# Feed-forward outputs: the last six chunks as plain products, block by block, and slots at multiples of 128 bytes

## The chip, the cores and the metric

The kernel runs on one core of a Trainium2 chip. The metric is device time in microseconds (us) of one execution. Three runs of the kernel before took 1276.67, 1276.96 and 1278.26 us; the median is 1276.96 us. One more execution was profiled, and all rows below come from it.

## The reference, cut to what matters

Two decoder layers work on 512 positions of width 1024. Layer 0 mixes with gated linear attention (GLA), layer 1 with a gated DeltaNet (GDN). Each layer ends with a gated feed-forward network (FFN) with a short causal convolution, and each sublayer closes with a scaled residual and a LayerNorm:

```python
def conv_ffn(x, w_in, conv_w, w_out):
    h = causal_dwconv(x @ w_in, conv_w)
    gate, up = jnp.split(h, 2, axis=-1)
    return (jax.nn.gelu(gate, approximate=False) * up) @ w_out

h = layer_norm(ALPHA * h + conv_ffn(h, ffn_w_in[i], ffn_conv_w[i], ffn_w_out[i]),
               ln_g[i, 1], ln_b[i, 1])
```

`w_in` is 1024 x 5632 and `w_out` 2816 x 1024, so the hidden width has 22 chunks of 128. Everything is float32.

## The kernel before, in words

Each float32 operand of a large product is split into a high part (rounded to the matmul format fp32r) and a low remainder. A product is then three matmuls: high by high, high by low, low by high. ScalarE writes the high part and VectorE the low part (`split_out`, L533). A 128x512 matmul of this kind is the unit of nearly all TensorE work here.

The 512 positions are four blocks of 128 (`tb` 0 to 3), and the width 1024 is two halves of 512 (`hf` 0 and 1), so the residual is eight tiles `h[tb][hf]`. The normed input stands transposed in `xh` and `xl`.

The FFN (`ffn`, L802) goes through the 22 hidden chunks in groups of 8, 8 and 6. Within a group, `fm_items` (L422) computes per chunk a gate and an up product, 24 matmuls each ("fm" in the trace). ScalarE and VectorE apply the convolution (`ffn_conv`, L794), the Gelu and the product with the gate. Then the group's part of the output product follows in `folded` (L850, "fold" in the trace): chunks are taken in pairs and the positions and the output width in halves, which makes each pair a 2x2 block product, and this is done with seven half-size products rather than eight. So a pair costs 7 forms x 2 row blocks x 3 terms = 42 matmuls. VectorE builds the four sums of activations (L831 to L834) and the sums of weights (L347), and seven updates (L877) add the products to the residual. The stationary operands are slices of tiles `fh` and `fl`, the moving ones the weight tiles `wh` and `wl`.

After the last group each residual block is normed as soon as both its halves are complete. In layer 0 that is `ln` (L689): statistics, two halves normed in place, eight transposes on TensorE ("xT"), then the new `xh` and `xl`. In layer 1 it is `ln_out` (L736), which scales and writes the output. The order of the seven products makes blocks 2 and 3 complete before 0 and 1. The next mixer therefore begins with the positions of blocks 2 and 3 (`self.halves = (1, 0)`, L908): its first four products (`HEADSTART`) are done for 256 positions at a time.

The instruction order on TensorE is written by a planner in the kernel: a model clock (`self.clk`) and background tasks that `pump` inserts when their time comes. Weights are taken from a plan list by `weight`, which prefetches as many items ahead as `self.look` says. Weights come through three buffers `raw` and are split into four pairs `wh`, `wl`, or, where the plan says so (`in_slots`), into free slots of the stage's own pool ("wsh", "wsl"). The mixers' output products (`out_proj`, L486) use that last way in their second half.

In SBUF the tiles `xh`, `xl`, `h`, `raw`, `wh` and `wl` begin at multiples of 128 bytes in each partition. The stage pools lie behind the constants, and their slots and the tiles `form`, `fh`, `fl` and `folded` begin 32 bytes past such a multiple.

Of the kernel before, what the change touches and what calls it, by code (L numbers as in the profile page):

```python
# [8 lines left out]
F32 = mybir.dt.float32  # L9
# [6 lines left out]
P = 128  # L16
# [44 lines left out]
class Trunk:  # L61
# [3 lines left out]
    def __init__(self, ctx, tc):  # L65
        self.tc = tc
        self.nc = nc = tc.nc
        self.n = 0
        ec = ctx.enter_context
        ap = ec(tc.tile_pool(name="acts", bufs=1))  # L70
        self.xh = ap.tile([P, NC, S], F32R, name="xh", tag="xh")
        self.xl = ap.tile([P, NC, S], F32R, name="xl", tag="xl")
        self.wp = ec(tc.tile_pool(name="wts", bufs=WB))
        self.hp = ec(tc.tile_pool(name="resid", bufs=2 * NTB))
        self.rp = ec(tc.tile_pool(name="raws", bufs=RAWB))
        self.cp = ec(tc.tile_pool(name="const", bufs=1))
        self.sp = ec(tc.tile_pool(name="small", bufs=4))
        self.pp = ec(tc.tile_pool(name="ps", bufs=8, space=bass.MemoryType.PSUM))
        self.dp = ec(tc.tile_pool(name="scratch", bufs=1, space=bass.MemoryType.DRAM))
        self.mp = None  # L80
        self.stage("gla", SLOTS)
        self.resets()
        self.halves = (0, 1)
        self.ident = self.keep([P, P], "ident")
        make_identity(nc, self.ident)
        ones = self.keep([P, 32], "one")
        self.one, self.warm, self.eps = (ones[:, i:i + 1] for i in range(3))
        nc.gpsimd.memset(ones, 1.0)
        nc.gpsimd.memset(self.eps, LN_EPS)
        self.h = None  # L90
        self.plan = []
        self.issued = 0
        self.loaded = 0
        self.taken = 0
        self.held = 0
        self.look = 1
        self.pin = True
        self.ready = []
        self.dve = 0.0
        self.clk = 0.0  # L100
        self.tasks = []
        self.flags = {}
        self.tabled = None
        self.wide = None
        self.block = None
        self.next_block = 0.0
        self.late = []
        self.first = None
        self.between = None

# [17 lines left out]

    def slot(self, s, dt=F32):
        return self.mp.tile([P, S], dt, name=self.uid(s), tag="slot")  # L130

    def psum(self, s):
        return self.pp.tile([P, S], F32, name=self.uid(s), tag="bank")
# [123 lines left out]
    def issue(self, item):  # L257
# [28 lines left out]
        if self.in_slots(item):  # L286
            w = []
            for j in range(used // S):
                wh, wl = self.slot("wsh", F32R), self.slot("wsl", F32R)
                nc.scalar.copy(wh, raw[:, blk(j, S)])  # L290
                nc.vector.tensor_sub(wl, raw[:, blk(j, S)], wh)
                self.vec(0.7)
                w.append((wh, wl))
            return w
# [127 lines left out]
    def fm_items(self, items):  # L422

        start = 0 if all(self.is_set(("x", tb)) for tb in range(NTB)) else HEADSTART
        first = items[:start]
        ws, banks = [], []
        for turn, half in enumerate(self.halves if first else ()):
            self.wait(("x", 2 * half), ("x", 2 * half + 1))
            for i, f in enumerate(first):
                if not turn:  # L430
                    ws.append(self.weight())
                    banks.append(self.psum("fm"))
                self.fm_mms(banks[i], ws[i], half * 256, half * 256 + 256, self.pin and not turn and i < 2)
                if turn:
                    self.spend()
                    f(banks[i])
        for f in items[start:]:
            w = self.weight()
            ps = self.psum("fm")
            self.fm_mms(ps, w, 0, S)  # L440
            self.spend()
            f(ps)
# [43 lines left out]
    def out_proj(self, a, n, first, final, pieces=1):  # L486
# [25 lines left out]
            self.tm_half(a, n, TAIL if last else 1, done, last, pieces if last else 1)  # L512
        self.look = LOOKAHEAD


    def exp_ln_table(self):
        load = self.nc.scalar.preload_act_table_set("natural_log_exp_and_others")
# [124 lines left out]

    def ln_consts(self, g, b):
        self.lg, self.lb = self.keep([P, 4 * NC], "lg"), self.keep([P, 4 * NC], "lb")
        self.specs = [(w.rearrange("i j (c p) -> (i j c) p", p=P), 4 * NC, t)
                      for w, t in ((g, self.lg), (b, self.lb))]

# [4 lines left out]
        for tb in range(NTB):  # L652
            self.flags.pop(("x", tb), None)

    def ln_gb(self):

        if self.gb is None:
            self.gb = []
            for src in self.gb_rows:
                for hf in range(2):  # L660
                    t = self.slot("gb")
                    self.nc.sync.dma_start(t, src[blk(hf, S)].partition_broadcast(P))
                    self.gb.append(t)
        return self.gb
# [115 lines left out]
    def ffn_plan(self, w_in, w_out):  # L780
        for f0, f1 in GROUPS:
            for f in range(f0, f1):
                self.plan_fm(w_in, f * P)
                self.plan_fm(w_in, DFF + f * P)
            self.plan_fold(w_out, f0, f1)

    def ffn_consts(self, conv_w):
        cw = self.keep([P, 6 * NF], "ffn_cw" + str(len(self.specs)))
# [13 lines left out]
    def ffn(self, cw, li, g, b, final, out=False):  # L802
        nc = self.nc
        self.stage(f"ffn{li}", FFN_SLOTS)
        for gi, (f0, f1) in enumerate(GROUPS):
            act, items, forms = {}, [], []
            for f in range(f0, f1):
                def gate(ps, f=f):
                    a = self.ffn_conv(ps, cw, f, self.slot("conv"))
                    nc.scalar.activation(a, a, AF.Gelu)  # L810
                    act[f] = a

                def up(ps, f=f, f1=f1):
                    odd = (f - f0) % 2
                    if not odd:
                        t = self.mp.tile([P, 2048], F32, name=self.uid("form"), tag="form", bufs=2)
                        forms.append((t, *(self.mp.tile([P, 1792], F32R, name=self.uid(n), tag=n, bufs=4)
                                           for n in ("fh", "fl"))))
                    t, fh, fl = forms[-1]
                    u = t[:, blk(odd, S)]  # L820
                    self.ffn_conv(ps, cw, NF + f, u)
                    nc.vector.tensor_mul(u, u, act.pop(f))
                    split = lambda lo, hi: self.split_out(fh[:, lo:hi], fl[:, lo:hi], t[:, 256 + lo:256 + hi])
                    if not odd:
                        if f + 2 == f1:
                            split(0, 256)
                        return
                    if f + 1 == f1:
                        split(256, 768)
                    part = lambda i: t[:, blk(i, 256)]  # L830
                    nc.vector.tensor_sub(part(4), part(0), part(2))  # L831
                    nc.vector.tensor_sub(part(5), part(4), part(1))
                    nc.vector.tensor_sub(part(6), part(1), part(0))
                    nc.vector.tensor_add(part(7), part(5), part(3))  # L834
                    if f + 1 == f1:
                        split(768, 1792)
                    else:
                        split(0, 1792)

                items += [gate, up]  # L840
            self.fm_items(items)
            last = gi == len(GROUPS) - 1
            if last:
                self.drain()
                self.ln_begin(li, g, b)
                if out:
                    self.ln_gb()
            self.folded(forms, gi == 0, final if last else None)

    def folded(self, forms, first, final):  # L850

        nc = self.nc
        m = len(forms)
        last = final is not None
        if last:
            self.sqrt_table()
        banks = [[self.psum("fold") for _ in range(2)] for _ in range(3)]
        uses = [[n for n, _, _, at in FOLD if at == i] for i in range(3)]  # L860
        fresh = {(tb, hf) for tb in range(NTB) for hf in range(2)} if first else set()
        st = {tb: self.small([P, 2, 6], "ln_st") for tb in range(NTB)} if last else None
        done = {}

        def update(name, r, ps):
            low, high = (r, 0), (r, 1)
# [9 lines left out]
            else:  # L876
                nc.vector.tensor_tensor(h, h, ps, op)  # L877
            self.vec(0.7, self.clk + 0.4)
            done[at] = done.get(at, 0) + 1
            if last and done[at] == (1 if at == low else 2):  # L880
                nc.vector.bn_stats(st[tb][:, hf, :], h)  # L881
                self.vec(0.7)
                if all(done.get((tb, i), 0) == (1 if (tb, i) == low else 2) for i in range(2)):
                    self.st = st
                    self.spawn(final(tb))
                    self.pump()

        self.look = 3
        for name, _, form, at in FOLD:
# [14 lines left out]
                    self.pump()  # L904
                self.spend()
        self.look = LOOKAHEAD
        if last:
            self.halves = (1, 0)  # L908


    def split_y(self, y, hf, sg):
# [241 lines left out]
    def mixer_out(self, y, li, g, b, final=None):  # L1153
# [5 lines left out]
            return tuple(t[:, blk(c % 4)] for t in y[tb][hf])  # L1159

        self.out_proj(a, NC, True, self.ln)
        self.halves = (0, 1)


    def gdn_plan(self, w_in, w_out):
# [475 lines left out]
```

## Time and profile before

| | |
|---|---|
| median of three runs | 1276.96 us |
| the profiled execution, its own time | 1277.17 us |
| its span, first to last instruction | 1275.5 us |
| TensorE busy | 1244.2 us, 98% |
| VectorE busy | 951.9 us, 75% |
| ScalarE busy | 594.7 us, 47% |
| granted TensorE clock, mean | 0.992 |

A matmul's row shows a duration that overlaps with the next one, so the rate of TensorE is read from the distance between starts, not from the durations. Times in the timeline and in the chain are counted from the span's start. "PEld" is the load of a stationary operand.

### The profile page before, as it was taken

Reading aid. Unit: us, or ns where it says so; the run is one execution under the profiler, and the core shown is the slowest. Engines: PE = TensorE matmul, PEld = TensorE weight load, DVE = VectorE, ACT = ScalarE, POOL = GpSimd, SP = SyncE. Lnnn points to the kernel's source line nnn. Section 1 sums busy time; section 2 is a strip of 40 time slices with the busy share of each in tenths; the row PEclk is TensorE's granted clock in tenths of the full one; section 3 lists DMA queues with packets and bytes.
Section 4 is the critical chain, followed back from the end, with each engine's and each line's share of the span. In section 5 each row is a group of like instructions: output and inputs, shape, how many; then the busy total and the mean of one; then the engine's idle time right before and its main releaser. Section 6 shows DMA issues by size and latency. Waiting matters only on the chain.

```text
span 1275.5 us, 17191 instructions
## 1 busy us (share of the span) xinstructions
PE 1244.2 (98%) x6520; PEld 1044.7 (82%) x6520; DVE 951.9 (75%) x1593; ACT 594.7 (47%) x1064; POOL 117.2 (9%) x152
## 2 busy tenths in 40 slices
PE   8999999999999999997999999999999999999994
PEld 8878888988888888877888888988988888888873
DVE  4953556689957895896789955679589966895798
ACT  4644444544434443446765544544644434443440
POOL 4000000080000000002013120010053000000000
PEclk9999999999999999998999999999999999999997
DMA  8321224442443144114354431145352253234301
GB/s 208 111 73 60 67 94 122 143 126 79 148 133 93 60 130 123 58 42 135 103 150 113 121 75 51 50 133 149 109 156 67 87 178 99 67 101 142 119 12 66
DMA packets 170307, 132.30 MB, mean 104 GB/s; under 512 B 16360, under 2 KB 140074, under 8 KB 170224
## 3 DMA queue, kind: packets, MB, share of 16 engines
q1 hardware_dynamic: 165136, 122.05, 32.5%
q0 software_dynamic: 3888, 8.50, 2.4%
q8 instruction: 51, 0.84, 0.3%
q10 hardware_dynamic: 1200, 0.66, 0.2%
q14 instruction: 32, 0.26, 0.1%
HBM read 125.39 MB, written 5.78 MB: 103 GB/s over the span
## 4 chain that ended last, share of the span: by engine, by line
PE 90%; DVE 7%; ACT 2%; issue 1%; DMA 0%; SPq 0%; DVEq 0%; ACTq 0%
PE fm L188 50%; PE tm L188 17%; PE fold L188 13%; DVE wl L534 2%; PE o L188 2%; PE xT L205 1%; DVE h L877 1%; PE R L188 1%; PE V L188 1%; PE qkT L205 1%; PE vn L188 1%; PE pq L188 1%; PE pg L188 1%; PE yT L205 1%; DVE ln_st L881 0%
## 5 line engine op out<-in xcount | busy, mean ns | idle before, releaser
L188 PE MATMUL fm<-xh,wh 128*128 128x512 f32 (+2 forms) x1104 | 403.1, 367 | 0.7 <-ACT xh L534 0.7
L188 PE MATMUL fm<-xl,wh 128*128 128x512 f32 (+2 forms) x1104 | 400.1, 365 | 0.0
L188 PE MATMUL fm<-xh,wl 128*128 128x512 f32 (+1 forms) x1088 | 396.3, 366 | 0.0
L534 DVE TENSOR_TENSOR wl<-raw,wh 128x1024 fp32r<-128x1024 f32 (+1 forms) x166 | 206.0, 1243 | 201.5 <-ACT wh L534 201.3
L534 ACT CAST wh<-raw 128x1024 fp32r<-128x1024 f32 (+1 forms) x166 | 172.8, 1042 | 291.1 <-PE fm L188 181.1
L188 PEld LDWEIGHTS fm<-xh,wh 128*128 128x128 f32 (+1 forms) x1104 | 207.3, 189 | 33.6 <-ACT xh L534 0.9
L188 PEld LDWEIGHTS fm<-xl,wh 128*128 128x128 f32 (+1 forms) x1104 | 207.4, 189 | 32.6
L188 PEld LDWEIGHTS fm<-xh,wl 128*128 128x128 f32 x1088 | 204.5, 189 | 33.4
L188 PE MATMUL fold<-wh,fh 128*128 128x512 f32 x308 | 122.5, 401 | 8.3 <-DVE ln_t L684 6.4
L188 PE MATMUL fold<-wl,fh 128*128 128x512 f32 x308 | 122.6, 398 | 0.0
L188 PE MATMUL fold<-wh,fl 128*128 128x512 f32 x308 | 122.5, 398 | 0.0
L534 ACT CAST wh<-b 128x1024 fp32r<-128x1024 f32 x72 | 69.2, 980 | 96.4 <-PE fold L188 40.0
L534 DVE TENSOR_TENSOR wl<-b,wh 128x1024 fp32r<-128x1024 f32 x72 | 80.2, 1129 | 4.6 <-ACT wh L534 4.4
L188 PE MATMUL tm<-wh,xh 128*128 128x512 f32 x192 | 78.5, 409 | 0.8 <-ACT qk L999 0.8
L188 PEld LDWEIGHTS fold<-wh,fh 128*128 128x128 f32 x308 | 58.1, 190 | 24.9 <-issue 6.8
L188 PE MATMUL tm<-wh,xl 128*128 128x512 f32 x192 | 75.3, 392 | 0.0
L188 PE MATMUL tm<-wl,xh 128*128 128x512 f32 x192 | 75.0, 391 | 0.0
L188 PEld LDWEIGHTS fold<-wl,fh 128*128 128x128 f32 x308 | 58.4, 189 | 14.2 <-DVE wl L534 0.5
L188 PEld LDWEIGHTS fold<-wh,fl 128*128 128x128 f32 x308 | 58.3, 189 | 14.1
L799 DVE SCALAR_TENSOR_TENSOR form<-fm,ffn_cw,form 128x511 f32<-128x511 f32 x88 | 65.6, 745 | 1.8 <-ACT form L797 0.4
L799 DVE SCALAR_TENSOR_TENSOR conv<-fm,ffn_cw,conv 128x511 f32<-128x511 f32 x88 | 65.5, 744 | 1.1
L810 ACT ACTIVATE conv<-conv 128x512 f32<-128x512 f32 x44 | 27.8, 631 | 78.6 <-DVE conv L799 78.5
(286 smaller groups left out, 1700.4 us busy)
## 6 DMA issues: line engine op xcount, KB each, us to landing
raw<-in_ffn_w_in_dram SPq DMA_DIRECT2D x88, 512.0 KB, 3.9
raw<-in_gdn_w_in_dram SPq DMA_DIRECT2D x32, 512.0 KB, 4.1
b<-in_ffn_w_out_dram SPq DMA_DIRECT2D x30, 512.0 KB, 5.0
raw<-in_gla_w_in_dram SPq DMA_DIRECT2D x23, 512.0 KB, 3.7
raw<-in_ffn_w_out_dram SPq DMA_DIRECT2D x20, 512.0 KB, 3.6
raw<-in_gla_w_out_dram SPq DMA_DIRECT2D x8, 512.0 KB, 3.6
raw<-in_gdn_w_out_dram SPq DMA_DIRECT2D x8, 512.0 KB, 3.9
h<-in_x_dram SPq DMA_DIRECT2D x8, 256.0 KB, 6.2
```

The lines of the kernel that those rows point to most:

```text
L188: t = self.nc.tensor.matmul(out, a, b, start=start, stop=stop, skip_group_check=joined)
L205: t = self.nc.tensor.transpose(out, a, self.ident[:n, :n])
L534: return self.nc.scalar.copy(dst_h, src), self.nc.vector.tensor_sub(dst_l, src, dst_h)
L799: nc.vector.scalar_tensor_tensor(a[:, d:], ps[:, :S - d], tap(2 - d), a[:, d:], ALU.mult, ALU.add)
L810: nc.scalar.activation(a, a, AF.Gelu)
L877: nc.vector.tensor_tensor(h, h, ps, op)
```

## The change

The seven-product form stays for the first two groups of eight chunks. The last six chunks are computed plainly: a new function `out_rows` goes block by block, and for each block over both output halves, with 6 chunks x 3 terms = 18 matmuls each, adds the result to the residual, takes the statistics and starts the block's LayerNorm. In layer 1 the very last half is done in two pieces of 256 columns. The twelve activations' parts and the 24 weight parts of this stage stand in slices ("rooms") of the tiles `fh`, `fl` and `folded` that the second group has left. The next mixer starts with blocks 0 and 1 again, as the blocks finish in order. In layer 1 the LayerNorm's scale and bias rows stand in a `form` tile. A constant of 24 floats is added ("pad"); with it and the changed small tiles, all stage pools begin at a multiple of 128 bytes.

```diff
+    def room(self, s):
+        return self.parts.pop(0) if self.parts else self.slot(s, F32R)
...
-                wh, wl = self.slot("wsh", F32R), self.slot("wsl", F32R)
+                wh, wl = self.room("wsh"), self.room("wsl")
...
+    def out_rows(self, a, n, final, pieces):
+        nc = self.nc
+        self.sqrt_table()
+        npair = (n + 1) // 2
+        self.look = 2 * npair + WB
+        ws = []
+        self.st = [None] * NTB
+        for tb in range(NTB):
+            for hf in range(2):
+                m = pieces if tb == NTB - 1 and hf else 1
+                ps = [self.psum("tm") for _ in range(m)]
+                while len(ws) < npair * (hf + 1):
+                    ws.append(self.weight())
+                w = [t for item in ws[npair * hf:npair * (hf + 1)] for t in item]
+                if hf == 0:
+                    self.st[tb] = self.small([P, 1 + (pieces if tb == NTB - 1 else 1), 6], f"ln_st{pieces}")
+                for i in range(m):
+                    cols = blk(i, S // m)
+                    for c in range(n):
+                        self.tm_terms(ps[i][:, cols], *a(c, tb), *(t[:, cols] for t in w[c]), c == 0, c == n - 1)
+                        if c % 2:
+                            self.pump()
+                    h = self.h[tb][hf][:, cols]
+                    nc.vector.tensor_add(h, h, ps[i][:, cols])
+                    nc.vector.bn_stats(self.st[tb][:, hf + i, :], h)
+                    self.vec(1.4, self.clk + 0.4)
+            self.spawn(final(tb))
+            self.pump()
+        self.look = LOOKAHEAD
...
         self.lg, self.lb = self.keep([P, 4 * NC], "lg"), self.keep([P, 4 * NC], "lb")
+        self.keep([P, 24], "pad")
...
-            self.plan_fold(w_out, f0, f1)
+            if f1 < NF:
+                self.plan_fold(w_out, f0, f1)
+            else:
+                for hf in range(2):
+                    for f in range(f0, f1, 2):
+                        self.plan_tm(w_out, f * P, min(2, f1 - f), hf * S, True)
...
+            if last:
+                self.parts = [t[:, blk(i, S)] for _ in range(4) for t in fine() for i in range(3)]
+                for _ in range(FOLDED):
+                    t = self.mp.tile([P, 1024], F32, name=self.uid("b"), tag="folded", bufs=FOLDED)
+                    self.parts += [t[:, blk(i, S)].bitcast(F32R) for i in range(2)]
...
+                def plain(ps, f=f, f1=f1):
+                    u = self.ffn_conv(ps, cw, NF + f, self.slot("conv"))
+                    nc.vector.tensor_mul(u, u, act.pop(f))
+                    t = self.room("gh"), self.room("gl")
+                    self.split_out(*t, u)
+                    forms.append(t)
+                    if f == f1 - 3:
+                        self.look = 5
+
+                items += [gate, plain if last else up]
...
+                a = lambda c, tb: tuple(t[:, blk(tb)] for t in forms[c])
+                self.out_rows(a, f1 - f0, final, 2 if out else 1)
+            else:
+                self.folded(forms, gi == 0)
...
-        if last:
-            self.halves = (1, 0)
```

More of the change, by code (lines that the diff above doesn't have):

```diff
@@ L82, in __init__ @@
         self.resets()
-        self.halves = (0, 1)
         self.ident = self.keep([P, P], "ident")
@@ L107, in __init__ @@
         self.late = []
+        self.parts = []
         self.first = None
@@ L426, in fm_items @@
         ws, banks = [], []
-        for turn, half in enumerate(self.halves if first else ()):
+        for turn, half in enumerate((0, 1) if first else ()):
             self.wait(("x", 2 * half), ("x", 2 * half + 1))
@@ L653, in ln_begin, with ln_gb @@
             self.flags.pop(("x", tb), None)
-    def ln_gb(self):
+    def ln_gb(self, room=None):
         if self.gb is None:
@@ L660, in ln_gb @@
                 for hf in range(2):
-                    t = self.slot("gb")
+                    t = room.pop(0) if room else self.slot("gb")
                     self.nc.sync.dma_start(t, src[blk(hf, S)].partition_broadcast(P))
@@ L804, in ffn @@
         self.stage(f"ffn{li}", FFN_SLOTS)
+        fine = lambda: tuple(self.mp.tile([P, 1792], F32R, name=self.uid(n), tag=n, bufs=4) for n in ("fh", "fl"))
         for gi, (f0, f1) in enumerate(GROUPS):
             act, items, forms = {}, [], []
+            last = gi == len(GROUPS) - 1
+            if last:
[3 more added lines that the diff above has]
+                    self.parts += [t[:, blk(i, S)].bitcast(F32R) for i in range(2)]
             for f in range(f0, f1):
@@ L816, in up @@
                         t = self.mp.tile([P, 2048], F32, name=self.uid("form"), tag="form", bufs=2)
-                        forms.append((t, *(self.mp.tile([P, 1792], F32R, name=self.uid(n), tag=n, bufs=4)
-                                           for n in ("fh", "fl"))))
+                        forms.append((t, *fine()))
                     t, fh, fl = forms[-1]
@@ L826, in up @@
                             split(0, 256)
[L827 to L836, printed above, removed]
-                    else:
-                        split(0, 1792)
-                items += [gate, up]
+                    else:
+                        if f + 1 == f1:
+                            split(256, 768)
+                        part = lambda i: t[:, blk(i, 256)]
+                        nc.vector.tensor_sub(part(4), part(0), part(2))
+                        nc.vector.tensor_sub(part(5), part(4), part(1))
+                        nc.vector.tensor_sub(part(6), part(1), part(0))
+                        nc.vector.tensor_add(part(7), part(5), part(3))
+                        split(768 if f + 1 == f1 else 0, 1792)
+                def plain(ps, f=f, f1=f1):
[7 more added lines that the diff above has]
+                items += [gate, plain if last else up]
             self.fm_items(items)
-            last = gi == len(GROUPS) - 1
             if last:
@@ L846, in ffn, with folded @@
                 if out:
-                    self.ln_gb()
-            self.folded(forms, gi == 0, final if last else None)
-    def folded(self, forms, first, final):
+                    t = self.mp.tile([P, 2048], F32, name=self.uid("form"), tag="form", bufs=2)
+                    self.ln_gb([t[:, blk(i, S)] for i in range(4)])
+                a = lambda c, tb: tuple(t[:, blk(tb)] for t in forms[c])
+                self.out_rows(a, f1 - f0, final, 2 if out else 1)
+            else:
+                self.folded(forms, gi == 0)
+        self.parts = []
+    def folded(self, forms, first):
         nc = self.nc
         m = len(forms)
-        last = final is not None
-        if last:
-            self.sqrt_table()
         banks = [[self.psum("fold") for _ in range(2)] for _ in range(3)]
@@ L861, in folded @@
         fresh = {(tb, hf) for tb in range(NTB) for hf in range(2)} if first else set()
-        st = {tb: self.small([P, 2, 6], "ln_st") for tb in range(NTB)} if last else None
-        done = {}
         def update(name, r, ps):
@@ L878, in update @@
             self.vec(0.7, self.clk + 0.4)
[L879 to L886, printed above, removed]
         self.look = 3
@@ L906, in folded @@
         self.look = LOOKAHEAD
-        if last:
-            self.halves = (1, 0)
     def split_y(self, y, hf, sg):
@@ L1161, in mixer_out @@
         self.out_proj(a, NC, True, self.ln)
-        self.halves = (0, 1)
     def gdn_plan(self, w_in, w_out):
```

## The prediction

> **What bounds the kernel now.** I read the page first, then the chain of waits, then windows around the stages that change, then the timeline at their edges.
>
> ```profile
> span 1275.5 us, 17191 instructions
> PE 1244.2 (98%) x6520; PEld 1044.7 (82%) x6520; DVE 951.9 (75%) x1593; ACT 594.7 (47%) x1064; POOL 117.2 (9%) x152
> PE 90%; DVE 7%; ACT 2%; issue 1%; DMA 0%; SPq 0%; DVEq 0%; ACTq 0%
> ```
>
> TensorE is busy for 98% of the span and holds 90% of the chain. So time goes in two ways only: fewer or quicker matmuls, or fewer of its few pauses. The chain gives the rate of a matmul of 512 columns as a run's length over its count.
>
> ```profile
> 994.09 33.59 PE fold L188 x144
> ...
> 1160.10 64.84 PE fm L188 x286
> ...
> 1257.27 5.59 PE fold L188 x15
> ...
> 1268.81 1.38 DVE h L749 x2
> ```
>
> An "fm" matmul takes 64.84 / 286 = 0.2267 us, a "fold" matmul of the same shape 33.59 / 144 = 0.2333 us. The two last rows show where the kernel ends: fifteen matmuls, and after them VectorE alone.
>
> The three windows are the last fold of layer 0 up to the next mixer's first product, the last fold of layer 1, and all that follows TensorE's end. The columns are length, TensorE busy time with its count, granted clock, DMA share and GB/s.
>
> ```profile
> 547.05:590.74 43.69, 35.70 (x159) 0.94 0.36 100
> 1224.78:1263.55 38.77, 32.16 (x127) 0.91 0.07 28
> 1263.55:1275.47 11.92, 0.00 (x1) 0.69 0.24 88
> ```
>
> Each of the first two holds 126 fold matmuls, which at 0.2333 would be 29.4 us. The first has 32 transposes besides. Here TensorE is idle for 8.0 and 6.6 us, and the clock falls below 1. The timeline of TensorE shows the pauses and what they cost afterwards.
>
> ```profile
> 587.41 3.68 PE L205 MATMUL xT<-ident,h 128*128 128x128 f32 x16 [5.71 <-DVE h L699]
> 590.74 0.56 PE L188 MATMUL fm<-xh,wh 128*128 128x256 f32 x1
> ...
> 592.73 0.28 PE L188 MATMUL fm<-xl,wh 128*128 128x256 f32 x1
> ...
> 596.45 0.28 PE L188 MATMUL fm<-xh,wl 128*128 128x256 f32 x1
> ...
> 1250.49 0.40 PE L188 MATMUL fold<-wh,fl 128*128 128x512 f32 x1
> 1257.27 0.77 PE L188 MATMUL fold<-wh,fh 128*128 128x512 f32 x1 [6.39 <-DVE ln_t L684]
> 1257.84 0.63 PE L188 MATMUL fold<-wl,fh 128*128 128x512 f32 x1
> 1258.27 0.63 PE L188 MATMUL fold<-wh,fl 128*128 128x512 f32 x1
> ```
>
> In layer 0 TensorE waits 5.71 us for a normed block. In layer 1 it waits 6.39 us while VectorE norms two blocks before it builds the last weights, and starts again 0.43 us apart, almost half rate. From 592.73 to 596.45 there are 31 steps of a 256-column matmul, 0.120 us each. From 590.74 to 592.73 there are 10 steps, 1.99 us, so the slow clock costs 0.8 us more behind the first window.
>
> **The change, part by part.** The sum is made against the profiled execution (1277.17 us, 1.7 above its span); the median of the runs is 0.2 lower.
>
> *Plain products instead of three pairs.* Six chunks x 8 tiles x 3 terms are 144 matmuls in a layer, where three pairs took 126. That is 18 more, 4.1 us a layer at 0.2267: by itself a loss, and all on the path. It is contained in the stage sums below.
>
> *Rate of the matmuls.* All slots move from 32 bytes past a multiple of 128 onto one. What could that do? Four groups differ in where the two operands lie: fm (both at 0) is at 0.2267, fold (stationary at 32, moving at 0) at 0.2333. The mixer's output product has the other two cases.
>
> ```profile
> 187.81 0.40 PE L188 MATMUL tm<-wh,yh 128*128 128x512 f32 x1
> ...
> 202.28 0.40 PE L188 MATMUL tm<-wh,yl 128*128 128x512 f32 x1
> 202.51 0.40 PE L188 MATMUL tm<-wsh,yh 128*128 128x512 f32 x1
> ...
> 215.89 0.39 PE L188 MATMUL tm<-wsh,yl 128*128 128x512 f32 x1
> ...
> 216.91 0.48 PE L188 MATMUL tm<-wsh,yh 128*128 128x512 f32 x1
> ```
>
> The first run has 63 starts: 14.47 / 62 = 0.2334, with `yh` in a slot (32) and `wh` outside (0). The second has 60: 13.38 / 59 = 0.2268, both in slots (32 and 32). The rate follows whether both operands have the same offset, so I take 0.2267 for all after the change. The counts:
>
> ```profile
> L188 PE MATMUL fold<-wh,fh 128*128 128x512 f32 x308 | 122.5, 401 | 8.3 <-DVE ln_t L684 6.4 <-ACT ln_root L677 1.5 <-ACT wh L534 0.4
> L188 PE MATMUL tm<-wh,yh 128*128 128x512 f32 x64 | 25.5, 398 | 0.0
> ```
>
> Three terms make 924 fold matmuls, of which 672 stay (11 pairs become 8), and 192 with `yh` or `yl` stationary. (672 + 192) x 0.0066 = 5.7 us less. The other end is nothing, since operands inside and outside the slots are also the ones far apart in memory, and no row separates the two readings. By the Trainium skill, "SBUF — State Buffer", section "Who interferes with whom", TensorE has two independent read ports, one for the moving operand and one for loading the stationary, and its section "Operand start alignment" calls alignment a matter of legality, not of speed. By that the 5.7 would be 0; the rows show a 3% difference that it doesn't explain.
>
> *Layer 0, last group.* Block by block, each block's LayerNorm has the next block's matmuls as cover. After the add, how long until its transposes can start? The same chain in the GLA mixer's end:
>
> ```profile
> 208.15 0.69 DVE L495 SCALAR_TENSOR_TENSOR h<-h,tm 128x512 f32<-128x512 f32 x1 [0.63 <-PE tm L188]
> ...
> 211.02 0.82 ACT L698 ACTIVATE h<-h,ln_nb,ln_rs 128x512 f32<-128x512 f32 x1 [0.87 <-DVE ln_nb L697]
> ```
>
> That is 3.7 us. In the changed order the first block's transposes stand behind 18 matmuls (4.1 us), those of the next two behind 24 (5.4 us), and those of the last behind 40 matmuls of 256 columns of the next mixer (4.8 us), which need blocks 0 and 1 alone. All are covered, the first by 0.4 us. Eight transposes take 216.91 - 215.89 - 0.23 = 0.79 us. The stage then costs 144 x 0.2267 + 4 x 0.79 = 35.8 us against 43.69: 7.9 less, and 0.8 less for the slow clock. If that cover failed, the pause would return at each block.
>
> *Layer 1, last group.* 126 matmuls of 512 and 36 of 256 columns: 28.6 + 4.3 = 32.9 us against 38.77: 5.9 less. VectorE's norm no longer stands ahead of weights that TensorE needs, since all weight parts but the last are split before the stage begins.
>
> *The stage's start* is new. TensorE needs the last chunk's activation after 15 matmuls, 3.4 us. The last chunk before:
>
> ```profile
> 1225.27 0.68 ACT L797 ACTIVATE form<-fm,ffn_cw 128x512 f32<-128x512 f32 x1
> ...
> 1226.01 1.53 DVE L799 SCALAR_TENSOR_TENSOR form<-fm,ffn_cw,form 128x511 f32<-128x511 f32 x2
> 1227.57 0.69 DVE L822 TENSOR_TENSOR form<-form,conv 128x512 f32<-128x512 f32 x1
> ...
> 1228.73 0.62 ACT L534 CAST fh<-form 128x512 fp32r<-128x512 f32 x1
> ...
> 1229.38 0.69 DVE L534 TENSOR_TENSOR fl<-form,fh 128x512 fp32r<-128x512 f32 x1
> ```
>
> From the stage's start (1224.78) the product ends at 3.5, so the high part can be there at 4.1 and the low one at 4.8. The changed order lets a few matmuls of the second half go first, so they are wanted at 3.9 and 4.5 to 5.0. In layer 0 a weight split for the next mixer (`wl` of 1024 columns) also stands ahead of the low part on VectorE:
>
> ```profile
> L534 DVE TENSOR_TENSOR wl<-raw,wh 128x1024 fp32r<-128x1024 f32 x162 | 203.2, 1256 | 197.5 <-ACT wh L534 197.3
> ```
>
> So I add 0.8 us in layer 0 and 0.4 in layer 1. The bounds are 0 and 2.0 a layer, the latter if the split's data also lands late. Ten loads go through three `raw` buffers there on SP's queue; behind a late one wait ScalarE's cast and, on its queue, the last chunk's own.
>
> *The end.* Before, two blocks are normed interleaved after the last matmul. After, one block is, and its last piece has 256 columns.
>
> ```profile
> 209.60 0.21 DVE L675 BATCH_NORM_AGGREGATE ln_mv<-ln_st 128x2 f32<-128x12 f32 x1
> ```
>
> ```profile
> 1265.69 1.40 DVE L742 SCALAR_TENSOR_TENSOR h<-h,ln_mv,gb 128x512 f32<-128x512 f32 x2
> ...
> 1271.61 0.48 DVE L749 SCALAR_TENSOR_TENSOR h<-h,ln_rs,gb 128x256 f32<-128x256 f32 x1
> ...
> 1272.12 0.37 ACTq L751 DMA_DIRECT2D out_dram<-h  x1
> ```
>
> ```profile
> out_dram<-h SPq DMA_DIRECT2D x7, 256.0 KB, 2.0
> ```
>
> Add and statistics of 256 columns at 0.48 each, the aggregate 0.21, centering 1.40, three short steps at about 0.18, scaling 1.4: 4.5 us. Then a write of 2.0 with 0.1 to issue it, and what the span has behind its last landing: 1275.47 - 1272.12 - 2.1 = 1.25. That is 7.9 against 11.92: 4.0 less. Bounds: 3 to 5.
>
> *At nothing:* the GLA stage and the first 16 chunks (same work), the moved `gb` loads (they land long before), VectorE's lighter last group (no sums of weights), and the pad. In the GDN stage TensorE has no pause to speak of; its order is written anew from another block order. I put it at 0, bounds -1 and +4.
>
> *Sum:* -5.7 - 7.9 - 0.8 - 5.9 + 1.2 - 4.0 = -23.1 us. That gives 1254.1 for a profiled execution and 1253.9 for the median; I say 1254.
>
> **The rivals.**
>
> *The slots' offset does nothing to the rate* (distance in memory does, or the pool). For it: the confounding named above, and the skill's page. Against it: four groups fall exactly by equal offset. The 5.7 us stay: 1259.6; if the plain products too ran at 0.2333, 288 x 0.0066 = 1.9 more, 1261.5.
>
> *The new stage starts late.* The last chunk, the casts and the ten loads crowd the last 10 us before it. At 2.0 to 4.0 us a layer instead of the 1.2 in all, TensorE also falls to the slow clock: 1257 to 1262. For it: the cover is short by my own count. Against it: the loads are planned four products ahead.
>
> *The GDN stage opens gaps, and the kernel is slower.* The place is its inverse and state chain, whose matmuls a model clock puts between the products. Its first products now take blocks 0 and 1, so all is shifted. If matmuls come before VectorE's work for them, TensorE stands. It decides from 23 us on, 8% of a stage of about 290 us that now pauses for less than 1 us: at 26 us, 1280. Against it: the same planner left no gap there before.
>
> **How the numbers follow.** The forecast has 0.62, the offset rival 0.17, the late start 0.14, the GDN gaps 0.05, of which a fraction remains faster; other mishaps 0.02. The likeliest is 1254. The range goes down by the bounds of end and start (1250) and up over both milder rivals (1262). Under 0.2%, 2.6 us, is about what a measurement here can't tell from no change. All cases but the last two lie far below that: faster 0.94, same 0.01, slower 0.05.
>
> **What would show it.** Right: 672 fold matmuls at 0.2267 and the `yh` run too; no pause over 1 us from the last group of layer 0 to the mixer, and full clock; windows of about 36.6 and 33.3 us for the two stages; 7.9 us behind the last matmul. Wrong: fold still at 0.2333; waits of the first "tm" matmuls for the last chunk or for weight parts; transposes waiting for `h`; pauses between 590 and 880 us.

## The result, and the profile after

Four runs of the changed kernel took 1256.79 to 1261.73 us, median 1260.88; four of the kernel before beside them 1276.67 to 1278.57, median 1277.61. The ratio is 0.9863 (95% interval 0.9839 to 0.9886). The kernel is faster by 16.7 us, where 23 were forecast, and the time lies inside the range given. The profiled execution took 1261.5 us, its span is 1259.8, against 1277.17 and 1275.5 before.

The windows of the changed kernel: first those that the prediction speaks of (last stage of layer 0, last stage of layer 1, all behind the last matmul), then the four folds that stay, then the GLA mixer's output product with what stands ahead of it, the GDN stage, and the GDN's output product. Columns: length, then the busy time of TensorE, of its weight loads, of VectorE, ScalarE and GpSimd with their counts, then granted clock, DMA share, GB/s.

```profile
545.09:585.82 40.73, 37.09 (x169) 30.50 (x168) 25.02 (x52) 19.02 (x40) 4.26 (x7) 0.96 0.29 82
1218.59:1251.86 33.27, 33.27 (x163) 27.76 (x161) 24.99 (x50) 4.63 (x8) 0.00 (x0) 1.00 0.13 48
1251.86:1259.79 7.93, 0.00 (x0) 0.00 (x0) 4.42 (x11) 0.29 (x1) 0.00 (x0) 0.73 0.18 66
315.97:354.98 39.01, 39.01 (x171) 31.75 (x170) 34.75 (x41) 17.14 (x18) 0.00 (x0) 1.00 0.50 158
441.57:480.27 38.70, 38.70 (x172) 31.83 (x170) 33.26 (x40) 16.78 (x17) 0.00 (x0) 1.00 0.24 69
988.37:1028.48 40.11, 39.02 (x171) 31.76 (x170) 35.85 (x44) 17.01 (x18) 0.00 (x0) 1.00 0.50 156
1115.07:1153.77 38.70, 38.70 (x172) 31.84 (x170) 33.25 (x40) 16.77 (x17) 0.00 (x0) 1.00 0.24 69
...
138.69:225.91 87.22, 87.22 (x411) 72.81 (x409) 53.36 (x107) 38.71 (x68) 0.00 (x0) 1.00 0.31 97
585.82:837.46 251.64, 251.24 (x1826) 219.69 (x1824) 184.92 (x470) 139.56 (x401) 41.14 (x78) 1.00 0.32 90
837.46:898.31 60.85, 60.85 (x287) 50.76 (x286) 51.10 (x112) 28.46 (x56) 0.00 (x0) 1.00 0.44 131
```

The same of the kernel before, from the four folds on:

```profile
316.19:355.88 39.69, 39.69 (x171) 31.86 (x170) 34.93 (x41) 17.21 (x18) 0.00 (x0) 1.00 0.51 157
442.50:482.19 39.69, 39.69 (x171) 31.86 (x170) 33.42 (x40) 16.77 (x17) 0.00 (x0) 1.00 0.43 126
993.93:1033.62 39.69, 39.69 (x171) 31.85 (x170) 34.95 (x41) 17.21 (x18) 0.00 (x0) 1.00 0.50 158
1120.24:1159.94 39.70, 39.70 (x171) 31.86 (x170) 33.43 (x40) 16.75 (x17) 0.00 (x0) 1.00 0.42 126
...
138.27:226.09 87.82, 87.82 (x410) 72.80 (x409) 53.35 (x107) 38.71 (x68) 0.00 (x0) 1.00 0.32 96
590.74:842.38 251.64, 251.25 (x1819) 219.63 (x1817) 184.72 (x463) 141.53 (x407) 38.40 (x73) 1.00 0.33 92
842.38:903.83 61.45, 61.45 (x287) 50.75 (x286) 51.38 (x112) 28.48 (x56) 0.00 (x0) 1.00 0.43 130
```

The last stage of layer 1 and the end came out as forecast (33.3 and 7.9 us), and the GDN stage keeps its 251.64 us. The last stage of layer 0 took 40.7 us where 36.6 were expected; the folds and output products gained 3.45 us in all where 5.7 were. One fold, the first of layer 1, gained nothing: 39.69 became 40.11.

### The profile page after: what moved, and what is told of

Its sections match the earlier page's. It is cut to its first block, busy times and chain, and to the rows that moved or that the text cites. A ratio compares the mean times of both kernels' runs of the same rounds, so it can differ in the third digit from the quotient of the medians.

```text
span 1259.8 us, 17201 instructions
## 1 busy us (share of the span) xinstructions
PE 1242.6 (99%) x6574; PEld 1050.7 (83%) x6574; DVE 914.2 (73%) x1541; ACT 584.2 (46%) x1062; POOL 115.1 (9%) x152
## 4 chain that ended last, share of the span: by engine, by line
PE 87%; DVE 8%; ACT 2%; DMA 2%; issue 1%; SPq 0%; DVEq 0%; ACTq 0%
PE fm L193 44%; PE tm L193 22%; PE fold L193 11%; DVE wl L571 2%; PE o L193 2%; PE xT L210 1%; DMA raw<-in_gdn_w_in_dram 1%; PE R L193 1%; DVE conv L842 1%; DVE form L842 1%; PE V L193 1%; PE qkT L210 1%; PE vn L193 1%; PE pq L193 1%; PE pg L193 1%
## 5 line engine op out<-in xcount | busy, mean ns | idle before, releaser
L193 PEld LDWEIGHTS fm<-xh,wl 128*128 128x128 f32 x1088 | 204.2, 189 | 33.3
L193 PE MATMUL fold<-wl,fh 128*128 128x512 f32 x224 | 87.4, 390 | 1.1 <-DVE wl L571 1.1
L193 PE MATMUL fold<-wh,fh 128*128 128x512 f32 x224 | 87.6, 391 | 0.0
L193 PE MATMUL fold<-wh,fl 128*128 128x512 f32 x224 | 87.2, 389 | 0.0
L842 DVE SCALAR_TENSOR_TENSOR conv<-fm,ffn_cw,conv 128x511 f32<-128x511 f32 x112 | 83.4, 745 | 5.1 <-ACT conv L840 3.7
L571 ACT CAST wh<-b 128x1024 fp32r<-128x1024 f32 x48 | 49.6, 1053 | 59.1 <-PE fold L193 25.8
L571 DVE TENSOR_TENSOR wl<-b,wh 128x1024 fp32r<-128x1024 f32 x48 | 57.8, 1216 | 2.3 <-ACT wh L571 2.3
L769 POOL TENSOR_TENSOR h<-h,gb 128x512 f32<-128x512 f32 x16 | 28.1, 1778 | 329.3 <-DMA gb<-in_ln_g_dram 329.3
L1237 DVE SCALAR_TENSOR_TENSOR conv<-fm,gdn_cw,conv 128x509 f32<-128x509 f32 (+2 forms) x72 | 53.2, 743 | 1.8 <-ACT conv L1235 1.0
L193 PEld LDWEIGHTS fold<-wl,fh 128*128 128x128 f32 x224 | 42.0, 188 | 10.5 <-DVE wl L571 1.9
L193 PEld LDWEIGHTS fold<-wh,fh 128*128 128x128 f32 x224 | 42.0, 188 | 9.8 <-DVE h L931 1.2
```

The lines of the kernel that those rows point to most:

```text
L193: t = self.nc.tensor.matmul(out, a, b, start=start, stop=stop, skip_group_check=joined)
L571: return self.nc.scalar.copy(dst_h, src), self.nc.vector.tensor_sub(dst_l, src, dst_h)
L769: nc.gpsimd.tensor_mul(h[hf], h[hf], gb[hf])
L842: nc.vector.scalar_tensor_tensor(a[:, d:], ps[:, :S - d], tap(2 - d), a[:, d:], ALU.mult, ALU.add)
L1237: self.conv = nc.vector.scalar_tensor_tensor(a[:, d:], ps[:, :S - d], tap(3 - d), a[:, d:], ALU.mult, ALU.add)
```

## The experiments

No kernel here leaves out any of the computation. Each ratio is to runs of the kernel before on the same chip in the same job. Differences between two changed kernels are taken across jobs, in which the kernel before has medians of 1277.05 to 1277.63 us.

**Is it the multiple of 128? The pad alone.** The kernel before with the pad that the change adds, and one with 32 bytes, so that the slots begin at a multiple of 128 and of 64:

```diff
         self.lg, self.lb = self.keep([P, 4 * NC], "lg"), self.keep([P, 4 * NC], "lb")
+        self.keep([P, 24], "pad")      # e1; in e4: [P, 8]
```

> The kernel before with the pad alone: all slots move to multiples of 128 bytes, and the last six chunks keep the seven products. By the theory of equal offsets the 924 fold matmuls go from 0.2333 to 0.2267 us and the 192 with yh or yl stationary too: 1116 x 0.0066 = 7.4 us, so about 0.994 of the time before (1270 us). VectorE may give some of it back where it builds the folds' sums, since these stages get shorter. By the rival (distance in memory, not offset) both rates stay and the time is that of before, 1.000.

> The kernel before with a pad of 32 bytes, so that slots begin 64 bytes past a multiple of 128, and the weights at a multiple. If the offset has to be equal within 128 bytes, the folds stay at 0.2333 and the time at that of before, 1.000. If 64 bytes are enough, the folds run at 0.2267 and it is the same as with the pad of 96 bytes, about 0.994.

Measured: 1276.76 us (1276.03 to 1277.78), ratio 0.9995 (0.9986 to 1.0003) for the multiple of 128, and 1276.95, 0.9995 (0.9986 to 1.0004) for the multiple of 64. Nothing was gained. A run of fold matmuls in the chain of the first:

```profile
442.85 33.47 PE fold L188 x144
```

33.47 / 144 = 0.2324 us, not 0.2267. So my reading "equal offset modulo 128" is wrong, although the changed kernel does run its folds at 0.2267:

```profile
441.73 32.64 PE fold L193 x144
```

**The other half: the plain products without the pad.**

```diff
-        self.keep([P, 24], "pad")
```

> The changed kernel without the pad: plain products block by block, but slots at 32 bytes past a multiple of 128. By equal offsets the 672 fold matmuls and the 192 with yh or yl are at 0.2333 again, 5.7 us more than the changed kernel (about 1266 us), while the 288 plain ones, both operands in slots, stay at 0.2267. By the rival of distance nothing moves: 1261 us and all folds at 0.2267.

Measured: 1264.9 us (1262.19 to 1267.04), ratio 0.9906 (0.9891 to 0.9921). Its folds are at 33.60 / 144 = 0.2333:

```profile
443.19 33.60 PE fold L193 x144
```

So by the medians the order of the last stage is worth 12.5 us, and the offset another 4.0, but in which unit does it count? The addresses of the tiles give it. The weight tiles `wh` and `wl` begin at 128 past a multiple of 256 bytes (a multiple of 128, as said above). The slots begin, in bytes past a multiple of 256, at 160 before, at 0 with the pad alone, at 192 with the small one, at 32 in the changed kernel without a pad, and at 128 in the changed kernel, whose small tiles differ from those of the kernel before. Only there are the two equal, modulo 256.

**The offset modulo 256, alone.** The kernel before with a pad that puts the slots 128 past a multiple of 256:

```diff
+        self.keep([P, 56], "pad")      # e6; in e7: [P, 120]
```

> The kernel before with one more constant of 56 floats (224 bytes): the stage pools move from 160 to 128 past a multiple of 256 bytes, where the tiles xh, xl, wh and wl also begin (they lie at 128 past a multiple of 256, and of 512). Nothing else changes. Theory A (the rate follows whether both operands have the same offset modulo 256): the fold starts are 0.2267 us apart, as in the changed kernel, and (924 fold + about 250 yh and yl) x 0.0066 us = 7.7 us are gained at most, a ratio of 0.994; some of it may come back as waits where VectorE is nearly the bound of the fold. Theory B (the changed kernel's faster fold comes from something other than the offsets): 0.2325 to 0.2333 us stay and the ratio is 1.000, as it was with 24 floats.

> The same with 120 floats (480 bytes): the pools begin at 384 past a multiple of 512, the weight tiles at 128 past one. The offsets are equal modulo 256 but not modulo 512. If 256 is the period, the fold runs at 0.2267 us a matmul and the ratio is that of the pad of 56 floats; if the period is 512 or more, 0.2325 us and a ratio of 1.000.

Measured: 1273.18 us (1272.76 to 1273.54), ratio 0.9964 (0.9952 to 0.9977), and 1273.15, 0.9963 (0.995 to 0.9977). The pitch is 32.64 / 144 = 0.2267 us in both:

```profile
441.83 32.64 PE fold L188 x144
```

```profile
441.37 32.64 PE fold L188 x144
```

The first is e6, the second e7. The period is thus 256 bytes. The gain is 4.5 us, not 7.7. The last folds of both layers show where it stays out, in e6:

```profile
545.23:588.86 43.63, 35.32 (x159) 28.11 (x158) 41.56 (x84) 25.82 (x46) 7.10 (x12) 0.93 0.36 100
1220.24:1259.91 39.67, 32.71 (x127) 25.23 (x125) 35.53 (x60) 12.62 (x17) 0.00 (x0) 0.87 0.07 27
```

Before, with the same columns, they were:

```profile
547.05:590.74 43.69, 35.70 (x159) 28.13 (x158) 41.56 (x84) 25.77 (x46) 7.09 (x12) 0.94 0.36 100
...
1224.78:1263.55 38.77, 32.16 (x127) 24.55 (x125) 35.55 (x60) 12.58 (x17) 0.00 (x0) 0.91 0.07 28
```

VectorE's 41.6 and 35.5 us of work are the same. A quicker TensorE there only waits longer for VectorE (8.3 us idle where it was 8.0, and 7.0 where it was 6.6), and in the second the clock (0.87 where it was 0.91) stays low for longer: 14 matmuls behind the pause start at about half rate, where it was 9, and the stage is even 0.9 us longer.

**Does the absolute address count?** A tile of 32 bytes ahead of all pools, so that activations, weights and slots all begin at 160 past a multiple of 256:

```diff
+        ec(tc.tile_pool(name="lead", bufs=1)).tile([P, 8], F32, name="lead", tag="lead")
...
+        self.keep([P, 56], "pad")
```

> The kernel before with a tile of 8 floats ahead of all pools and the pad of 56 floats: activations, weights and stage slots all begin at 160 past a multiple of 256 bytes, so that nothing lies on a multiple of 64 and all offsets are equal. If only the difference of the two operands' offsets counts, the fold and the fm matmuls are 0.2267 us apart and the ratio is that of the pad of 56 floats (0.994). If the multiple of 128 itself counts, every matmul is slower: fold and fm at 0.2325 us or more, and 2300 fm matmuls x 0.0066 us = 15 us lost or more, a ratio of 1.012.

Measured: 1272.94 us (1272.39 to 1274.4), ratio 0.9965 (0.9952 to 0.9979). Folds and "fm" products run at 32.64 / 144 and 64.61 / 285, 0.2267 both:

```profile
441.39 32.64 PE fold L189 x144
...
1155.00 64.61 PE fm L189 x285
```

So the difference of the two offsets counts; neither operand has to lie on a multiple of 64 or 128.

**Where layer 0 lost its time.** The start of the changed kernel's last stage, TensorE, then ScalarE, then VectorE:

```profile
545.09 0.39 PE L193 MATMUL tm<-fh,fh 128*128 128x512 f32 x1
...
552.75 1.22 PE L193 MATMUL tm<-fh,b 128*128 128x512 f32 x2 [3.64 <-ACT b L571]
553.76 0.63 PE L193 MATMUL tm<-fl,fh 128*128 128x512 f32 x1
554.19 1.05 PE L193 MATMUL tm<-b,fh 128*128 128x512 f32 x2
555.04 0.63 PE L193 MATMUL tm<-fh,b 128*128 128x512 f32 x1
```

```profile
547.56 1.05 ACT L571 CAST wh<-raw 128x1024 fp32r<-128x1024 f32 x1 [2.85 <-DMA raw<-in_gdn_w_in_dram]
548.52 0.68 ACT L840 ACTIVATE conv<-fm,ffn_cw 128x512 f32<-128x512 f32 x1
549.17 1.04 ACT L571 CAST wh<-raw 128x1024 fp32r<-128x1024 f32 x1
552.08 0.62 ACT L571 CAST b<-conv 128x512 fp32r<-128x512 f32 x1 [1.86 <-DVE conv L888]
```

```profile
548.65 1.23 DVE L571 TENSOR_TENSOR wl<-raw,wh 128x1024 fp32r<-128x1024 f32 x1 [3.53 <-ACT wh L571]
549.79 1.53 DVE L842 SCALAR_TENSOR_TENSOR conv<-fm,ffn_cw,conv 128x511 f32<-128x511 f32 x2
551.35 0.69 DVE L888 TENSOR_TENSOR conv<-conv,conv 128x512 f32<-128x512 f32 x1
```

The last chunk's product ends at 545.1, but ScalarE begins its convolution only at 548.52. Ahead of it in the queue stands the cast of a weight tile for the next mixer (`in_gdn_w_in`), and ScalarE waits 2.85 us for its load. VectorE stands 3.53 us behind that cast too. The chain that ended last goes through the same load:

```profile
541.97 5.57 DMA raw<-in_gdn_w_in_dram
...
552.75 10.13 PE tm L193 x37
```

TensorE stands 3.64 us and starts again at half rate (0.43 us a matmul from 554.19 to 555.47). My theory: the cause is the place of the next mixer's loads and casts ahead of the last chunk's own work. The rival: the chain of the last chunk alone is too long, as the prediction's own count had it. The test issues the next mixer's four early weight tiles, in the program, behind the second block, and orders their casts behind that block's norm (`self.normed` holds the two instructions that norm a block):

```diff
-            split(pieces[0])
+            for ins, other in zip(split(pieces[0]), self.hold or ()):
+                self.behind(ins, other)
...
-        self.look = 2 * npair + WB
...
+                    self.look = 2 * npair - len(ws) - 1
...
+            if tb == 1:
+                self.hold, self.look = self.normed, WB
+                self.prefetch()
+                self.hold = None
```

> The changed kernel, with the four first weight tiles of the next mixer issued after the second block of the row stage and their split ordered behind that block's norm, on ScalarE and VectorE. By the theory of the queue (in layer 0 ScalarE's cast of such a weight stands ahead of the last chunk's convolution and waits for its transfer) the pause of 3.64 us and the slow clock behind it go: the pause is under 0.5 us and the time 5 us less, about 1256. By the rival of the long last chunk (its own six steps are too slow) the pause stays at 3.6 us: 1261. If the wait only moves, the first products of the next mixer wait for their weights instead, and the time stays at 1261 too.

Measured: 1255.77 us (1255.3 to 1256.11), ratio 0.9829 (0.9815 to 0.9842): 5 us below the changed kernel by the medians. The last stage of layer 0, the first fold of layer 1 and the last stage of layer 1, then ScalarE at the start of the first of them:

```profile
544.64:580.64 36.00, 35.77 (x169) 29.28 (x168) 25.84 (x52) 19.50 (x38) 4.25 (x7) 1.00 0.35 99
983.21:1022.25 39.04, 39.02 (x172) 31.75 (x171) 34.78 (x41) 17.12 (x18) 0.00 (x0) 1.00 0.51 160
1212.36:1245.62 33.26, 33.26 (x163) 27.76 (x161) 24.99 (x50) 4.62 (x8) 0.00 (x0) 1.00 0.13 48
```

```profile
544.85 0.69 ACT L846 ACTIVATE conv<-fm,ffn_cw 128x512 f32<-128x512 f32 x1 [2.46 <-PE fm L194]
547.86 0.62 ACT L577 CAST b<-conv 128x512 fp32r<-128x512 f32 x1 [2.33 <-DVE conv L894]
```

The convolution now starts as its product ends, the high part is ready 3.8 us after the stage's start (548.48 - 544.64), and TensorE goes on: 36.0 us at full clock instead of 40.7. The rival falls: the chain itself fits. The first two of the next mixer's loads still start ahead of the stage (533.8 and 537.3 us) and the others inside it (551.8 and 568.2), but none of their casts stands ahead of the last chunk any more: the first runs at 565.8.

How much of the loss was the load's own 5.57 us? In the kernel without the pad, the same stage starts at 547.61, the load is issued at 544.15 and lands at 548.24. The stage, ScalarE and then TensorE read:

```profile
547.61:585.12 37.51, 35.74 (x170) 29.43 (x168) 25.00 (x51) 19.05 (x40) 4.25 (x7) 1.00 0.30 87
```

```profile
548.26 1.05 ACT L571 CAST wh<-raw 128x1024 fp32r<-128x1024 f32 x1 [1.36 <-DMA raw<-in_gdn_w_in_dram]
549.21 0.68 ACT L839 ACTIVATE conv<-fm,ffn_cw 128x512 f32<-128x512 f32 x1
```

```profile
553.44 0.73 PE L193 MATMUL tm<-fh,b 128*128 128x512 f32 x2 [1.77 <-ACT b L571]
```

There the load took 4.1 us, TensorE paused 1.77 us, its clock stayed full, and the stage took 37.5 us. So a load of 4.1 us is late as well, and the one of 5.57 us came with a stage 3.2 us longer. The profile of the kernel without the pad is of its fastest run (1262.19 us); its three others took 1264.65 to 1267.04.

**A single last piece in layer 1, and the offset again.** The best kernel so far with the very last half in one piece:

```diff
-                self.out_rows(a, f1 - f0, final, 2 if out else 1)
+                self.out_rows(a, f1 - f0, final, 1)
```

> The changed kernel with the next mixer's loads behind the second block's norm (as in the run named e5_loads_behind) and, in layer 1, the very last half in one piece of 512 columns instead of two of 256. 36 matmuls of 256 columns (4.3 us) become 18 of 512 (4.1 us), but add, statistics and scaling at the end take 512 columns. Add and statistics at 0.69 instead of 0.48 each, so about 0.4 us more behind the last matmul: 8.3 instead of 7.9 us, and the sum is +0.2 us against e5_loads_behind. If the half pieces were what took the 4 us off the end, it would be 2 us or more.

Measured: 1260.05 us (1259.52 to 1261.09), ratio 0.9863 (0.9849 to 0.9876): 4.3 us more, not 0.2. The last stage and the end do what was expected (33.00 and 8.44 us, against 33.26 and 7.93), so that is not where the time is:

```profile
1216.92:1249.92 33.00, 33.00 (x145) 26.70 (x143) 24.25 (x48) 4.63 (x8) 0.00 (x0) 1.00 0.13 48
1249.92:1258.36 8.44, 0.00 (x1) 0.00 (x0) 4.93 (x11) 0.29 (x1) 0.00 (x0) 0.72 0.17 62
```

The folds show where it is:

```profile
442.84 33.47 PE fold L194 x144
```

33.47 / 144 = 0.2324 again: one small tile of statistics fewer, and the slots begin at a multiple of 256, where the weights do not. The same with 56 floats of pad, beside the kernel with two pieces run once more:

```diff
-        self.keep([P, 24], "pad")
+        self.keep([P, 56], "pad")
```

> One piece of 512 columns in layer 1's last half, as in the run named e9_one_piece, but with 56 floats of pad instead of 24. Without the half pieces the last block's statistics need one small tile fewer, and the stage pools had moved to a multiple of 256 bytes, where the weights are not; with 56 floats they are at 128 past one again, as the weights are. Theory (e9 lost its 4 us to the offset alone): fold at 0.2267 us again, and a time 0.2 to 0.5 us above the kernel with half pieces measured beside it. Rival (the single piece itself costs the 4 us): 1260 us stay.

> The kernel of e5_loads_behind once more, beside the one with a single last piece: 1255.8 us expected, as before, and without the scatter of the changed kernel (1256.8 to 1261.7), whose 5 us I put down to when the third weight load lands. If the runs spread over 4 us here too, the scatter is not of that load.

Measured: 1256.0 us (1255.47 to 1256.46), ratio 0.9832 (0.9819 to 0.9845), with one piece; 1255.77 (1254.97 to 1256.23), 0.9831 (0.9817 to 0.9844), with two. The fold is at 0.2267 again,

```profile
441.76 32.64 PE fold L194 x144
```

and the halved last piece is worth 0.2 us by the medians, within the runs' spread. The eight runs with the loads behind lie within 1.3 us, where the four of the changed kernel spread over 4.9; that fits the late load, though the single runs have no trace. Their mean clocks go the same way: 0.998 in the fastest run of the changed kernel (1256.79 us), 0.996 to 0.997 in the others.

## Why the prediction was right or wrong

The spans differ by 15.7 us (1275.5 and 1259.8); the sum had 23.1. Term by term, gains counted as negative:

| term | forecast | measured |
|---|---|---|
| rate by offset | -5.7 | -3.45 |
| layer 0, last group and start (-7.9 + 0.8) | -7.1 | -2.96 |
| layer 1, last group and start (-5.9 + 0.4) | -5.5 | -5.50 |
| the end | -4.0 | -3.99 |
| GDN stage: the slow clock at its start (-0.8), no new gaps (0) | -0.8 | 0.00 |

The rest is +0.42 in the first 140 us (138.27 and 138.69 in the rows above) and -0.20 spread over the "fm" products of the FFNs (the times between those rows).

*Plain products block by block* was right, in its mechanism and its size. TensorE has no pause of note at layer 0's transposes, and layer 1's stage holds 33.27 us of work in 33.27 us, at full clock. LayerNorm's cover held. (Of the 0.4 us given to the start in layer 1, the starts show about 0.2: the first 23 steps take 5.42 us where 23 x 0.2267 is 5.21. That the term fits to 0.01 us is luck.)

*The stage's start, layer 0*, is the step that failed. The prediction named the cause ("behind a late one wait ScalarE's cast and, on its queue, the last chunk's own"), but priced it as a bound of 2.0 us and chose 0.8; it measured 3.6, and some 2 more went mostly to the slow clock: the stage took 40.7 where 144 x 0.2267 and three sets of transposes make 35.0. I added the split on VectorE as a queue delay and didn't follow the load chain: the third load is issued only when VectorE frees a `raw` buffer, 3 us ahead of the stage (541.97), and takes 4.1 to 5.6 us. One subtraction in the trace after shows it: 541.97 + 4.1 = 546.1, against a product that ends at 545.1. The profile page of the kernel before gives the 4.1 us for such a load; the time of its issue would have had to be worked out from the plan of loads. The rival "the new stage starts late" (0.14) was therefore what took place in layer 0, and its 2.0 to 4.0 us and slow clock were right; in layer 1, with no next mixer, there was no such pause.

*The slow clock's 0.8 us at the mixer* is not seen as a gain: the stage keeps its 251.64 us. Its first matmuls do run at full rate, 0.12 us apart, but the eight transposes of the last block, whose 0.79 us I had counted in the sum of the stage ahead, now stand in it:

```profile
590.85 1.03 PE L210 MATMUL xT<-ident,h 128*128 128x128 f32 x8
```

*The rate* was right by chance. The mechanism (the difference of the offsets) stands, but the period is 256 bytes and not 128, and no row of the trace before could tell these apart, since 32 past is unequal in both. With the kernel before's small tiles, the same 24 floats of pad gain nothing. The size was off as well: the folds gained 0.7, 1.0, -0.4 and 1.0 us instead of 1.1 each, the output products 0.6 each as forecast. The -0.4 holds a wait for a low part of the weights:

```profile
1008.90 0.50 PE L193 MATMUL fold<-wl,fh 128*128 128x512 f32 x1 [1.09 <-DVE wl L571]
```

VectorE has 33.3 to 35.9 us of work in a fold of 39 us, in bursts. At 0.2267 TensorE catches up with it by a little: at this matmul it comes about 0.2 us too early in e5 as well (its start there is 0.41 us behind the one ahead of it), and the first fold of a layer takes 39.0 us where the second takes 38.7. The long pause is another matter. It is in the changed kernel and in one of the two runs with the loads behind (1.0 us in e11), not in the other, and e4 has one at the same place at 0.2333:

```profile
1014.20 0.50 PE L188 MATMUL fold<-wl,fh 128*128 128x512 f32 x1 [0.66 <-DVE wl L534]
```

So the pitch alone doesn't bring it, and what does stays open. I had costed the rate as if every matmul's saving reached the end.

By the Trainium skill, "SBUF — State Buffer", section "Who interferes with whom", the port for the moving operand and that for the stationary are independent, and TensorE never waits on anyone. That rule would have made the offset worth nothing. The runs e6, e7 and e8 differ: 0.2267 against 0.2324 to 0.2333 us, by offset alone, and the measurement decides. The prediction also took the remark on start alignment as a ground for 0; that remark is about what is legal, and says nothing of the rate.

*The end* came out as worked, and the GDN stage opened no gaps.

## What to carry to other kernels

When work for the next stage is prefetched, follow each of its loads from the buffer that it waits for to the cast that it holds up, and ask what critical work stands behind that cast in the same engine's queue; moving such casts behind the critical work gained 5 us here. Put the two operands of matmuls like these at the same offset modulo 256 bytes, and look at the pitch again after every edit that changes a small tile, because it shifts all that lies behind it. A quicker engine gains only where its partner has slack: the 3% of pitch was worth nothing in the last folds of the kernel before, which VectorE bounds.

## What the runs showed of the hardware

The pitch of 128x512 fp32r matmuls depends on the distance of the two operands' addresses modulo 256 bytes: 0.2267 us at 0 (the changed kernel, e5 to e8, e10, e11), 0.2324 at 128 (e1, e9), 0.2333 at 32, 64 and 160 (before, e4 and e2). Here is the row of e4:

```profile
442.70 33.60 PE fold L188 x144
```

What in the chip does this isn't known from these runs.

TensorE's clock fell to half behind a pause of 3.64 us (starts 0.43 us apart) and stayed full behind one of 1.77. The Trainium skill, "TensorE: Matmul & The Clock Gate", section "Part 1: The HAM clock gate", puts the step at an idle window of about 3.4 us; these two pauses lie on either side of it and agree.
